# A two-block transformer kernel on one Trainium2 core: the second block's output projection as seven half-size products, its gated mix by token halves

## Chip, core and metric

The kernel runs on one core of one Trainium2 chip. The metric is the device time of one execution in microseconds (us). The engines have names in the profile: PE is TensorE (matmuls), PEld its weight loads, DVE is VectorE, ACT ScalarE, POOL GpSimd, and SP is the engine whose queue issues most of the DMAs. "L80" is line 80 of the kernel file.

## What is computed

Two blocks run one after the other on a sequence of 1024 tokens with 1024 channels, all in float32. The first block has a windowed attention layer and a multiscale pooling layer. The second has, in front of its tokens, 16 meta tokens, then a mixer of two branches, a gated mix, an output projection and an MLP. What concerns the change is this part of the reference:

```python
y_na = neighbourhood_attention(...) @ w_na_out[l]
y_hg = hgrn2_branch(...) @ w_hg_out[l]
mix = jax.nn.sigmoid(gate_na) * y_na + jax.nn.sigmoid(gate_hg) * y_hg
h = h + mix @ w_o[l]
m = rms_norm(h, norm_mlp[l])
h = h + jnp.square(jax.nn.relu(m @ w_up[l])) @ w_down[l]
```

`w_hg_out` is 512 x 1024 and `w_o` is 1024 x 1024.

## The kernel before

**Products.** A float32 product is made of three fp32r matmuls. Each operand is split into a high part (a cast on ACT) and a low part (the original minus the high part), and `mm3` adds high x high, high x low and low x high into one PSUM bank. Low parts of activations are made on DVE (`split_evac`, L118 and L119); low parts of weights on POOL (`split_w`, L79 the cast, L80 the subtraction). A raw weight tile (`wraw`), its high part (`whi`) and its low part (`wlo`) have 128 x 1024 elements and three buffers each.

**The gated mix.** `mixed(e)` makes two of the eight 128-channel blocks of the mix, transposed (channels on partitions), for all tokens. `pair_cols` loads two column blocks of `w_hg` and splits them. For each block and each half of 512 tokens, two pieces of 256 KB are loaded from DRAM into a slot of the tile `fa`: the sigmoid gate (`d_gate`) and the finished first term (`d_y`). Twelve matmuls make the second branch's output in a PSUM bank; DVE multiplies it by the gate (L1359), adds the first term (L1360), and ACT and DVE split the sum into `mh` and `ml`.

**The output projection.** `add_out` multiplies the blocks of the mix by two row blocks of `w_o` at a time and adds each 128 x 512 result to the residual `X` (L539; the first time the residual is also scaled by `rfin`, L541). `X` is two tiles, `Xa` for rows 0 to 3 of 128 tokens and `Xb` for rows 4 to 7. So the two kinds of work alternate: mix of blocks 0 to 3, projection of 0 and 1, mix of 4 and 5, projection of 2 and 3, mix of 6 and 7, and at last the projection of 4 to 7, first for `Xa`, then for `Xb`, for which `w_o`'s rows 4 to 7 are loaded and split a second time. `last_hook` stores finished rows to `d_x` (L1372), and beside the last quarter it makes the norm of rows 0 to 3 and turns them for the MLP.

**After it** the MLP's up projection starts (`first_two`, sums of operands at L1519 and L1533, the seven-product scheme), with the norms of rows 4 to 7 in two pairs (`norms`, L1322 to L1328). The MLP's down projection is written with the helpers `load_d`, `less`, `split_a`, `split_b`, `times` and `into` (L1643 to L1696).

**What sets the order.** Each engine executes its instructions in one fixed order, and each DMA queue in its own. That order comes from the program and from a scheduler that places instructions by their dependences and estimated times; an instruction waits for the semaphores of its inputs and of the buffer that it overwrites, and whatever is queued behind it on its engine waits too.

Of the kernel before, what the change touches and what calls it, by code (L numbers as in the profile page):

```python
# [9 lines left out]
F32 = mybir.dt.float32  # L10
# [9 lines left out]
P = 128  # L20
# [10 lines left out]
def fused_kernel(tc, a, out, stop=None, dbg=None):  # L31
# [4 lines left out]
    def f(x):  # L36
        return x.bitcast(F32)
# [1301 lines left out]
    with ExitStack() as ph:  # L1339
        gp = ph.enter_context(tc.tile_pool(name="gp", bufs=2))  # L1340
        sgs = itertools.count()

        def mixed(e):

            mx, wh = [], pair_cols(w_hg, e)
            for i in range(2):
                m_h = gp.tile([P, T], F32R, name="mh", bufs=4)
                m_l = gp.tile([P, T], F32R, name="ml", bufs=4)
                mx.append((m_h, m_l))
                for hf in range(2):  # L1350
                    sl = slice(hf * 512, hf * 512 + 512)
                    sg = []
                    for src in (d_gate[8 + e + i], d_y[e + i]):
                        g_ = fa[:, next(sgs) % 8, :]
                        nc.sync.dma_start(out=g_, in_=src[:, sl])
# [3 lines left out]
                    nc.vector.tensor_tensor(out=sg[0], in0=ps, in1=sg[0], op=ALU.mult)  # L1359
                    nc.vector.scalar_tensor_tensor(out=sg[0], in0=sg[1], scalar=0.5, in1=sg[0], op0=ALU.mult,  # L1360
                                                   op1=ALU.add)
# [45 lines left out]

    def copy_out(ps):  # L1410
# [19 lines left out]
    def load_d(dst, j, n, c):  # L1430
        for i in range(2):
            q = 4 * c + 2 * i
            loads[:] = [nc.sync.dma_start(out=dst[i], in_=wd[:, q:q + 2, j, n * 512:n * 512 + 512])]
        return dst

    def load_w11(c):
        return load_d([wpool.tile([P, 1024], F32, name="wraw", bufs=3).rearrange("p (k c) -> p k c", k=2)
                       for _ in range(2)], 0, 0, c)

    def load_w2(c):  # L1440
        wx = xt.tile([P, KT, 512], F32, name="xh1")
        w12, w22 = [[wx[:, 4 * n + 2 * i:4 * n + 2 * i + 2, :] for i in range(2)] for n in range(2)]
        load_d(w22, 1, 1, c)
        load_d(w12, 0, 1, c)
        return w12, w22

    blocks = [fa[:, 0:4, :], fa[:, 4:8, :]]
    loads, stores = [None], []

    with ExitStack() as ph:  # L1450
# [17 lines left out]
        def first_two(p, w_):  # L1468
# [3 lines left out]
            u11 = copy_out(b_)  # L1472
# [89 lines left out]
        def pair(p, r1, r2, tt=None):  # L1562
# [45 lines left out]
        w11 = load_w11(0)  # L1608
# [3 lines left out]
    with ExitStack() as ph:  # L1612
# [36 lines left out]
        def load_w21(c):  # L1649
            return load_d([bb.tile([P, 2, 512], F32, name="wb") for _ in range(2)], 1, 0, c)  # L1650
# [5 lines left out]
        def less(out_, x_, y_):  # L1656
            for i in range(2):
                nc.vector.tensor_tensor(out=out_[i], in0=x_[i], in1=y_[i], op=ALU.subtract)  # L1658

        def split_a(n):  # L1660
            t_ = xt.tile([P, KT, 512], F32R, name=("xh0", "xl0", "xl1")[n % 3])
            for i in range(2):
                h, l = t_[:, 2 * i:2 * i + 2, :], t_[:, 4 + 2 * i:6 + 2 * i, :]
                split_evac(h, l, blocks[n % 3][:, 2 * i:2 * i + 2, :])
# [3 lines left out]
        def split_b(b_):
            res = []
            for i in range(2):  # L1670
                hi = wpool.tile([P, 1024], F32R, name="whi").rearrange("p (k c) -> p k c", k=2)
                lo = wpool.tile([P, 1024], F32R, name="wlo").rearrange("p (k c) -> p k c", k=2)
                split_evac(hi, lo, b_[i], nc.gpsimd)
                res.append((hi, lo))
            return res

        def times(banks, s_, w_, first, by_t=False):
            for i, t in [(i, t) for t in range(4) for i in range(2)] if by_t else [(i, t) for i in range(2) for t in range(4)]:
                tsl = slice(t * P, (t + 1) * P)
                mm3(banks[t], [((s_[:, 2 * i + k, tsl], s_[:, 4 + 2 * i + k, tsl]), (w_[i][0][:, k, :], w_[i][1][:, k, :]))  # L1680
                               for k in range(2)], first and i == 0, i == 1, chain=True)
# [92 lines left out]
```

## Time and profile before

| what | value |
| --- | --- |
| three runs | 2376.79, 2378.60, 2380.87 us (median 2378.6) |
| profiled execution | 2379.78 us |
| its span, first to last instruction | 2378.0 us |
| mean granted TensorE clock | 0.994 |
| matmuls | 12102 |
| DMA traffic | 168.68 MB read from HBM, 59.24 MB written |

The page has the span in 40 slices, with each engine's busy share in tenths:

```profile
PE   7999999999999999999999999999989999999997
DVE  5566676654367255553265746767684444786775
ACT  5344452422226454553232232421365555533334
POOL 2112133112126244431212112112354444444455
```

A 9 is 90% or more. One slice is 59.5 us; the changed stage, from the mix to the end of the output projection (1591 to 1735 us), lies in slices 27 to 30.

### The profile page before, as it was taken

To read this page: it belongs to the slowest core of one execution; us is meant where nothing else is said; L and a number is where in the kernel's file an instruction comes from. 1 tells how busy PE (TensorE), PEld (TensorE's weight loads), DVE (VectorE), ACT (ScalarE), POOL (GpSimd) and SP (SyncE) were. 2 spreads that over 40 slices of the span, in tenths; PEclk is the share of its full clock that TensorE was granted. 3 is DMA by queue.
4 is the path that set the end of the run, shared out by engine and by line. 5 is a ranking of instruction groups with operands and counts; after the bars stand their busy time and mean duration, and the time that the engine had idled before them with its cause. 6 is when DMAs were issued, how large, how long until landed. Compare 5 with 4: busy or idle time off the path is not lost. (4 is left out here: it accounts for less than half of the span.)

```text
span 2378.0 us, 32146 instructions
## 1 busy us (share of the span) xinstructions
PE 2317.6 (97%) x12102; PEld 1929.5 (81%) x12102; DVE 1409.7 (59%) x2623; ACT 961.9 (40%) x1788; POOL 762.4 (32%) x516
## 2 busy tenths in 40 slices
PE   7999999999999999999999999999989999999997
PEld 6877777888887888878988888878867888878886
DVE  5566676654367255553265746767684444786775
ACT  5344452422226454553232232421365555533334
POOL 2112133112126244431212112112354444444455
PEclk9999999999999999999999999999999999999999
DMA  5111003111114222211111111465335444754231
GB/s 160 36 28 36 28 27 108 40 45 58 40 59 136 68 67 67 54 58 45 45 53 54 41 54 54 136 217 200 133 102 199 147 150 164 274 213 173 102 124 72
DMA packets 234012, 230.02 MB, mean 97 GB/s; under 512 B 59832, under 2 KB 174862, under 8 KB 230272
## 3 DMA queue, kind: packets, MB, share of 16 engines
q1 hardware_dynamic: 225040, 210.31, 27.7%
q10 hardware_dynamic: 8224, 16.00, 1.8%
q0 software_dynamic: 592, 1.65, 0.3%
q8 instruction: 96, 1.57, 0.3%
q14 instruction: 60, 0.49, 0.1%
HBM read 168.68 MB, written 59.24 MB: 96 GB/s over the span
## 5 line engine op out<-in xcount | busy, mean ns | idle before, releaser
L108 PE MATMUL mm<-xh,whi 128*128 128x512 f32 (+2 forms) x1744 | 671.7, 385 | 8.4 <-DVE st L1418 2.5
L110 PE MATMUL mm<-xl,whi 128*128 128x512 f32 (+2 forms) x1744 | 666.2, 382 | 0.0
L111 PE MATMUL mm<-xh,wlo 128*128 128x512 f32 (+2 forms) x1744 | 662.4, 380 | 1.6 <-POOL wlo L80 1.6
L80 POOL TENSOR_TENSOR wlo<-wraw,whi 128x1024 fp32r<-128x1024 f32 (+1 forms) x135 | 319.8, 2374 | 949.1 <-ACT whi L79 910.4
L108 PEld LDWEIGHTS mm<-xh,whi 128*128 128x128 f32 x1744 | 329.5, 189 | 70.6 <-issue 4.2
L111 PEld LDWEIGHTS mm<-xh,wlo 128*128 128x128 f32 x1744 | 329.6, 189 | 65.6 <-POOL wlo L80 2.7
L110 PEld LDWEIGHTS mm<-xl,whi 128*128 128x128 f32 x1744 | 329.7, 189 | 56.4 <-DVE xl L119 0.3
L79 ACT CAST whi<-wraw 128x1024 fp32r<-128x1024 f32 (+1 forms) x135 | 137.4, 1022 | 386.1 <-PE mm L110 159.9
L111 PE MATMUL mm<-whi,xl 128*128 128x512 f32 (+1 forms) x624 | 221.4, 355 | 0.0
L108 PE MATMUL mm<-whi,xh 128*128 128x512 f32 (+1 forms) x496 | 172.1, 347 | 2.4 <-DVE X L281 1.6
L110 PE MATMUL mm<-wlo,xh 128*128 128x512 f32 (+1 forms) x496 | 171.9, 347 | 1.6 <-POOL wlo L119 1.0
L111 PEld LDWEIGHTS mm<-whi,xl 128*128 128x128 f32 x624 | 117.8, 189 | 16.6
L1553 POOL TENSOR_TENSOR wlo<-raw,whi 128x1024 fp32r<-128x1024 f32 (+1 forms) x42 | 84.3, 2007 | 101.9 <-ACT whi L1552 101.9
L108 PE MATMUL mm<-whi,xl 128*128 128x512 f32 x288 | 112.3, 390 | 1.5 <-ACT whi L118 1.1
L110 PE MATMUL mm<-wlo,xl 128*128 128x512 f32 x288 | 112.1, 389 | 0.0
L108 PEld LDWEIGHTS mm<-whi,xh 128*128 128x128 f32 x496 | 93.7, 189 | 14.5 <-DVE X L281 2.0
L110 PEld LDWEIGHTS mm<-wlo,xh 128*128 128x128 f32 x496 | 93.7, 189 | 13.5 <-POOL wlo L119 1.4
L111 PE MATMUL mm<-whi,ml 128*128 128x512 f32 x256 | 99.7, 392 | 1.6 <-DVE ml L119 1.6
L108 PE MATMUL mm<-whi,mh 128*128 128x512 f32 x256 | 100.4, 392 | 0.1
L110 PE MATMUL mm<-wlo,mh 128*128 128x512 f32 x256 | 99.9, 390 | 0.0
L1479 DVE TENSOR_TENSOR st<-st 128x512 f32<-128x512 f32 x64 | 63.2, 1008 | 58.0 <-ACT st L1465 56.9
L1696 DVE TENSOR_TENSOR X<-X,mm 128x512 f32<-128x512 f32 x112 | 73.1, 681 | 37.4 <-PE mm L111 37.4
(344 smaller groups left out, 4362.6 us busy)
## 6 DMA issues: line engine op xcount, KB each, us to landing
wraw<-in_w_in_dram SPq DMA_DIRECT2D x48, 512.0 KB, 3.9
d_S<-st SPq DMA_DIRECT2D x64, 256.0 KB, 4.6
raw<-in_w_up_dram SPq DMA_DIRECT2D x30, 512.0 KB, 5.4
d_A<-st ACTq DMA_DIRECT2D x48, 256.0 KB, 2.0
fa<-d_S SPq DMA_DIRECT2D x10, 1024.0 KB, 5.4
wraw<-in_pool_w_in_dram SPq DMA_DIRECT2D x18, 512.0 KB, 4.1
fa<-d_A SPq DMA_DIRECT2D x9, 1024.0 KB, 4.9
wraw<-in_attn_w_in_dram SPq DMA_DIRECT2D x32, 256.0 KB, 3.3
```

Of the source, the lines that this page charges most:

```text
L79: nc.scalar.copy(out=hv[:, i:i + n], in_=view[:, i:i + n])
L80: nc.gpsimd.tensor_tensor(out=lv[:, i:i + n], in0=view[:, i:i + n], in1=f(hv[:, i:i + n]), op=ALU.subtract)
L108: nc.tensor.matmul(ps, lhsT=lh[0], rhs=rh[0], start=first and i == 0, stop=False, skip_group_check=chain)
L110: nc.tensor.matmul(ps, lhsT=lh[0], rhs=rh[1], start=False, stop=False, skip_group_check=chain)
L111: nc.tensor.matmul(ps, lhsT=lh[1], rhs=rh[0], start=False, stop=last and i == n - 1, skip_group_check=chain)
L1479: return nc.vector.tensor_tensor(out=out_, in0=x_, in1=y_, op=op)
L1553: nc.gpsimd.tensor_tensor(out=lv, in0=view, in1=f(hv), op=ALU.subtract)
L1696: added[:] = [nc.vector.tensor_tensor(out=dst, in0=dst, in1=banks[t], op=ALU.add)]
```

## The change

The mix keeps its arithmetic, but is made by token halves: `mixed(e, hf)` makes two channel blocks for 512 tokens, for all e of the first half and then of the second, so the pairs of `w_hg` are loaded and split eight times, not four. The gate and the first term go into slots of one staging tile (`stb`, ten slots, also used by the MLP), and the sum goes to a place where it stays: `fa` for the first token half, the new tiles `a21` and `a22` for the second.

The output projection is then one 2 x 2 block product by the seven-product scheme (Strassen's, in Winograd's form with chained sums): tokens, inner channels and output channels are halved, and the four quarters of the mix and of `w_o` (w11, w12, w21, w22, 512 x 512 each) are combined by additions before, and by chained PSUM sums after. Each of the seven products takes 48 matmuls. The helpers of the MLP's down projection are moved up and shared (`load_d`, `less`, `split_b`, `times`, and `split_into` for operand splits on ACT and DVE). The sums of activations are made by `block` on DVE, one of them (a21 + a22) on POOL. `add_x` adds finished quarters to `X`; `summed` stores finished rows; the norm of rows 0 to 3 stands between products 5 and 6 in the text, and their turning (`turn`) between the row tiles of the seventh product. `load_x` loads the residual's rows after some of the mix's steps. The other edits pass arguments for the shared helpers and the staging slot that a pair of the MLP holds.

```diff
-    def stage():
-        return st.tile([P, 512], F32, name="st", bufs=10)
+    stb = st.tile([P, 10, 512], F32, name="st")
+    def stage(hold=None):
+        i = next(i for i in (n % 10 for n in sts) if i not in held.values())
...
+    def split_b(b_):
+        res = []
+        for i in range(2):
+            hi, lo = [wpool.tile([P, 1024], F32R, name=n).rearrange("p (k c) -> p k c", k=2) for n in ("whi", "wlo")]
+            split_evac(hi, lo, b_[i], nc.gpsimd)
+            res.append((hi, lo))
+        return res
...
-        def mixed(e):
-            mx, wh = [], pair_cols(w_hg, e)
+        a21, a22, w12, w22 = [mp.tile([P, 4, 512], F32, name=n) for n in ("a21", "a22", "w12", "w22")]
+        mix = {(0, 0): fa[:, 0:4, :], (0, 1): fa[:, 4:8, :], (1, 0): a21, (1, 1): a22}
+        def mixed(e, hf):
+            wh, sl = pair_cols(w_hg, e), slice(hf * 512, hf * 512 + 512)
             for i in range(2):
...
-                    split_evac(m_h[:, sl], m_l[:, sl], sg[0])
+                g_, y_ = stage(), stage()
+                nc.sync.dma_start(out=g_, in_=d_gate[8 + e + i][:, sl])
+                nc.sync.dma_start(out=y_, in_=d_y[e + i][:, sl])
+                ps, m_ = bank(), mix[hf, i][:, e // 2, :]
+                mm3(ps, [(wh[i][k], oo.at(4 + k, sl)) for k in range(4)])
+                nc.vector.tensor_tensor(out=m_, in0=ps, in1=g_, op=ALU.mult)
+                nc.vector.scalar_tensor_tensor(out=m_, in0=y_, scalar=0.5, in1=m_, op0=ALU.mult, op1=ALU.add)
+        def add_x(banks, h, ch, first=True):
+            for t in range(4 * h, 4 * h + 4):
+                dst, ps = X[ALL, t, slice(ch * 512, ch * 512 + 512)], banks[t - 4 * h]
+                if first:
+                    nc.vector.scalar_tensor_tensor(out=dst, in0=dst, scalar=rfin[:, t:t + 1], in1=ps, op0=ALU.mult,
                                                    op1=ALU.add)
+                else:
+                    nc.vector.tensor_tensor(out=dst, in0=dst, in1=ps, op=ALU.add)
+                if h and not ch:
+                    summed(t)
...
-        m0 = mixed(0)
-        m1 = mixed(2)
...
-        add_out(psm, terms(m0), wo(0), scale=rfin)
-        m0 = mixed(4)
-        add_out(psm, terms(m1), wo(2), by_ch=True)
-        m1 = mixed(6)
-        for hf in range(2):
...
-            add_out(psm, terms(m0), wo(4), tiles=tiles, by_ch=True)
-            w6 = wo(6)
...
-            add_out(psm, terms(m1), w6, last_hook, tiles=tiles)
+        s2, w21 = stb[:, 0:4, :], halves(stb[:, 4:8, :])
+        for e in range(0, KT, 2):
+            mixed(e, 0)
+            if e >= 4:
+                load_d(w22 if e == 4 else w12, wv, int(e == 4), 1)
+        a11, a12 = mix[0, 0], mix[0, 1]
+        o11 = split_a("xh0", halves(a11))
+        mixed(0, 1)
+        load_x(0, 1)
+        o12 = split_a("xl0", halves(a12))
+        mixed(2, 1)
+        load_x(2, 3)
+        mixed(4, 1)
+        w11 = load_w11(wv)
+        mixed(6, 1)
+        load_d(w21, wv, 1, 0)
+        load_x(4, 5, 6, 7)
+        ops = split_b(w11)
+        B, A_ = banks4(), banks4()
+        block(a11, a21, a11, ALU.subtract)
+        times(B, o11, ops, True)
+        ops = split_b(w21)
+        block(a21, a21, a22, ALU.add, nc.gpsimd)
+        less(w12, w12, w22)
+        block(s2, a22, a11, ALU.add)
+        add_x(B, 0, 0)
+        times(A_, o12, ops, True)
+        less(w11, w11, w12)
+        o22 = split_a("xh1", halves(a22))
+        ops = split_a("xl1", halves(s2)), split_b(w11)
+        less(w21, w21, w11)
+        less(w11, w22, w11)
+        add_x(A_, 0, 0, False)
+        times(B, *ops, False)
+        ops = split_a("xh0", halves(a21)), split_b(w11)
+        block(a12, a12, s2, ALU.subtract)
+        add_x(B, 0, 1)
+        C = banks4()
+        times(C, *ops, True)
+        ops = split_a("xl0", halves(a12)), split_b(w22)
+        add_x(C, 1, 1)
+        times(C, *ops, False)
+        ops = split_a("xl1", halves(a11)), split_b(w12)
...
+        add_x(C, 0, 1, False)
+        for t in range(4):
+            summed(t)
+        norms(0, 4)
+        times(B, *ops, False, True)
+        wu0 = load_w(cols(w_up, 0))
+        add_x(B, 1, 1, False)
+        for t, ks in enumerate(((0, 1, 2), (3, 4, 5), (6, 7), ())):
+            times(B, o22, t4, False, True, [t])
+            for k in ks:
+                turn(k)
+        wu0 = split_w(wu0.rearrange("p (k c) -> p k c", k=KT), [KT, P])
+        add_x(B, 1, 0)
```

The lines that the next paragraphs name are, in the changed kernel: L60 a weight load, L1404 and L1405 the loads of gate and first term, L1408 and L1409 the two operations of the mix, L1358 a load of `w_o`, L1367 `less`, L1416 and L1419 `add_x`, L1438 `load_x`, L1448 `block`.

SP's queue at the start of the mix. Before, the loads for the mix (`fa`, L1355) stand between the last stores of the first term (`d_y`, L1240):

```order
L60 DMA wraw<-in_w_hg_out_dram 128x4x128 x2
L1236 DMA gate<-d_gate 128x512
L1240 DMA d_y<-gate 128x512 x2
L1355 DMA fa<-d_gate 128x512
L1240 DMA d_y<-gate 128x512
L1355 DMA fa<-d_y 128x512
L1355 DMA fa<-d_gate 128x512
```

and in the changed kernel (`st` is a slot of the staging tile):

```order
L60 DMA wraw<-in_w_hg_out_dram 128x4x128 x2
L1236 DMA gate<-d_gate 128x512
L1240 DMA d_y<-gate 128x512 x4
L60 DMA wraw<-in_w_hg_out_dram 128x4x128 x2
L1404 DMA st<-d_gate 128x512
L1405 DMA st<-d_y 128x512
L1404 DMA st<-d_gate 128x512
```

All four stores come first now, and another pair of `w_hg` stands ahead of the mix's first load. Further on in the same queue of the changed kernel stand `w12` (here with a number as `w_14792`), the rows of `Xa`, and the `w_hg` pair of e = 4 for the second token half:

```order
L1358 DMA w_14792<-in_w_o_dram 128x2x512 x2
L1404 DMA st<-d_gate 128x512
L1405 DMA st<-d_y 128x512
L1404 DMA st<-d_gate 128x512
L1405 DMA st<-d_y 128x512
L1438 DMA Xa<-d_h 128x1024 x2
L1404 DMA st<-d_gate 128x512
L1405 DMA st<-d_y 128x512
L1404 DMA st<-d_gate 128x512
L1405 DMA st<-d_y 128x512
L1438 DMA Xa<-d_h 128x1024 x2
L60 DMA wraw<-in_w_hg_out_dram 128x4x128 x2
```

That pair now stands behind `w22`, `w12`, four rows of `Xa` and the pieces of twelve of the sixteen products of the mix.

POOL's order from the mix on. Before, it has nothing but low parts of weights up to the MLP's sums (L1532):

```order
L1113 TENSOR_TENSOR kc<-K 128x512 x2
L80 TENSOR_TENSOR wlo<-wraw,whi 128x1024 x6
L1113 TENSOR_TENSOR kc<-K 128x512 x2
L80 TENSOR_TENSOR wlo<-wraw,whi 128x1024 x23
L1532 TENSOR_TENSOR fa<-xh_15758,xl_15759 128x512 x4
```

and in the changed kernel (`a_14790` is `a21`, `a_14791` is `a22`, `w_14793` is `w22`):

```order
L80 TENSOR_TENSOR wlo<-wraw,whi 128x1024 x12
L1448 TENSOR_TENSOR a_14790<-a_14790,a_14791 128x1024
L80 TENSOR_TENSOR wlo<-wraw,whi 128x1024 x2
L119 TENSOR_TENSOR wlo<-wraw,whi 128x1024 x2
L119 TENSOR_TENSOR wlo<-st,whi 128x1024
L1448 TENSOR_TENSOR a_14790<-a_14790,a_14791 128x1024
L119 TENSOR_TENSOR wlo<-st,whi 128x1024
L119 TENSOR_TENSOR wlo<-wraw,whi 128x1024 x4
L119 TENSOR_TENSOR wlo<-w_14793,whi 128x1024 x2
```

The first half of a21 + a22 now stands between the low parts of the first six `w_hg` pairs and those of the last two (e = 4 and e = 6 of the second token half).

DVE's order in the mix. Before, each block's product, sum and low part follow one another:

```order
L1359 TENSOR_TENSOR fa<-mm,fa 128x512
L1360 SCALAR_TENSOR_TENSOR fa<-fa 128x512
L119 TENSOR_TENSOR ml<-fa,mh 128x512
L1359 TENSOR_TENSOR fa<-mm,fa 128x512
L1360 SCALAR_TENSOR_TENSOR fa<-fa 128x512
```

and in the changed kernel, from the seventh sum of the first token half on (`xh_14962` and `xl_15010` are the split halves of the mix for products 1 and 2):

```order
L1409 SCALAR_TENSOR_TENSOR fa<-st,fa 128x512
L1367 TENSOR_TENSOR w_14792<-w_14792,w_14793 128x1024
L1408 TENSOR_TENSOR fa<-mm,st 128x512
L119 TENSOR_TENSOR xh_14962<-fa,xh_14962 128x1024
L1409 SCALAR_TENSOR_TENSOR fa<-st,fa 128x512
L119 TENSOR_TENSOR xh_14962<-fa,xh_14962 128x1024
L1408 TENSOR_TENSOR a_14790<-mm,st 128x512
L119 TENSOR_TENSOR xl_15010<-fa,xl_15010 128x1024
L1409 SCALAR_TENSOR_TENSOR a_14790<-st,a_14790 128x512
L1408 TENSOR_TENSOR a_14791<-mm,st 128x512
L119 TENSOR_TENSOR xl_15010<-fa,xl_15010 128x1024
```

The subtraction w12 - w22 now stands ahead of the eighth product's operations, and low parts of twice the width lie between the products.

More of the change, by code (lines that the diff above doesn't have):

```diff
@@ L1311, in bank @@
         return psm.tile([P, 512], F32, name="mm")
-    def stage():
-        return st.tile([P, 512], F32, name="st", bufs=10)
+    stb = st.tile([P, 10, 512], F32, name="st")
+    sts, held = itertools.count(), {}
+    def stage(hold=None):
+        i = next(i for i in (n % 10 for n in sts) if i not in held.values())
+        if hold is not None:
+            held[hold] = i
+        return stb[:, i, :]
     def norms(t0, n):
@@ new lines, in fused_kernel, with load_d, load_w11, less @@
+    added, loads = [None], [None]
+    def load_d(dst, w, j, n, c=0):
+        for i in range(2):
+            q = 4 * c + 2 * i
+            loads[:] = [nc.sync.dma_start(out=dst[i], in_=w[:, q:q + 2, j, n * 512:n * 512 + 512])]
+        return dst
+    def load_w11(w, c=0):
+        return load_d([wpool.tile([P, 1024], F32, name="wraw", bufs=3).rearrange("p (k c) -> p k c", k=2)
+                       for _ in range(2)], w, 0, 0, c)
+    def less(out_, x_, y_):
+        for i in range(2):
+            nc.vector.tensor_tensor(out=out_[i], in0=x_[i], in1=y_[i], op=ALU.subtract)
@@ new lines, in split_into, with times @@
+    def split_into(t_, parts):
+        for i in range(2):
+            split_evac(t_[:, 2 * i:2 * i + 2, :], t_[:, 4 + 2 * i:6 + 2 * i, :], parts[i])
+        return t_
+    def split_b(b_):
+        res = []
+        for i in range(2):
+            hi, lo = [wpool.tile([P, 1024], F32R, name=n).rearrange("p (k c) -> p k c", k=2) for n in ("whi", "wlo")]
+            split_evac(hi, lo, b_[i], nc.gpsimd)
+            res.append((hi, lo))
+        return res
+    def times(banks, s_, w_, first, by_t=False, rows=range(4)):
+        for i, t in [(i, t) for t in rows for i in range(2)] if by_t else [(i, t) for i in range(2) for t in rows]:
+            tsl = slice(t * P, (t + 1) * P)
+            mm3(banks[t], [((s_[:, 2 * i + k, tsl], s_[:, 4 + 2 * i + k, tsl]), (w_[i][0][:, k, :], w_[i][1][:, k, :]))
+                           for k in range(2)], first and i == 0, i == 1, chain=True)
@@ L1442, in load_w2 @@
         w12, w22 = [[wx[:, 4 * n + 2 * i:4 * n + 2 * i + 2, :] for i in range(2)] for n in range(2)]
-        load_d(w22, 1, 1, c)
-        load_d(w12, 0, 1, c)
+        load_d(w22, wd, 1, 1, c)
+        load_d(w12, wd, 0, 1, c)
         return w12, w22
     blocks = [fa[:, 0:4, :], fa[:, 4:8, :]]
-    loads, stores = [None], []
+    stores = []
     with ExitStack() as ph:
@@ L1599, in pair @@
                 store(order)
+            held.pop(p)
             return n1, n2
@@ L1654, in load_x @@
                 nc.sync.dma_start(out=X[:, t, ch * 512:ch * 512 + 512], in_=d_x[t][:, ch * 512:ch * 512 + 512])
-        def less(out_, x_, y_):
-            for i in range(2):
-                nc.vector.tensor_tensor(out=out_[i], in0=x_[i], in1=y_[i], op=ALU.subtract)
         def split_a(n):
[L1661 to L1664, printed above, removed]
+            t_ = split_into(xt.tile([P, KT, 512], F32R, name=("xh0", "xl0", "xl1")[n % 3]),
+                            [blocks[n % 3][:, 2 * i:2 * i + 2, :] for i in range(2)])
             load_a(n + 3)
             return t_
[L1668 to L1681, printed above, removed]
         w21 = load_w21(0)
@@ L1708, in fused_kernel @@
             n, last = 7 * c, c == NCH - 1
-            B, A_ = [[bank() for _ in range(4)] for _ in range(2)]
+            B, A_ = banks4(), banks4()
             times(B, *ops, True)
@@ L1722, in fused_kernel @@
             into(B, 0, 1)
-            C = [bank() for _ in range(4)]
+            C = banks4()
             times(C, *ops, True)
```

86 lines of the change are left out of this document (33 added, 53 removed).

## The prediction

> **What bounds the kernel now.** I read the page's totals first, then the windows by stage, then the waits of TensorE, and last the timeline of single engines around the gated mix.
>
> ```profile
> span 2378.0 us, 32146 instructions
> PE 2317.6 (97%) x12102; PEld 1929.5 (81%) x12102; DVE 1409.7 (59%) x2623; ACT 961.9 (40%) x1788; POOL 762.4 (32%) x516
> ...
> 1591.00:1667.00 76.00, 75.97 (x333) 62.53 (x334) 51.56 (x67) 13.61 (x19) 16.76 (x7) 1.00 0.62 214
> ...
> 1610.00:1620.00 10.00, 10.00 (x45) 8.26 (x44) 8.49 (x11) 2.82 (x4) 2.39 (x1) 1.00 1.01 379
> ```
>
> TensorE (PE) is the bound: 97% of the span, and without a gap in the changed stage from 1591 to 1667 us. There one matmul takes 75.97/333 = 0.228 us. The last two figures of a window's row are the DMA share and GB/s: at share 1.01 the engines are full, and 379 GB/s is what full means here.
>
> ```profile
> PE mm L1336 <- DVE xl L1519: 2.3, 1, 2.3
> PE mm L1336 <- DVE Xb L1328: 1.5, 1, 1.5
> PE mm L1336 <- DVE st L1418: 0.9, 1, 0.9
> PE mm L108 <- DVE gate L1239: 0.9, 1, 0.9
> PE mm L108 <- ACT st L1522: 0.9, 1, 0.9
> PE mm L111 <- POOL wlo L80: 0.5, 1, 0.5
> ```
>
> Those are all waits of PE from 1590 to 1760. Only the 0.9 at L1239 (before the mix) and the tail behind the output projection (L1328, L1519, L1418, L1522, together 5.6) exist. Whatever the change saves in matmuls is thus real time, unless a new wait appears.
>
> **What the change saves.** The projection has 384 matmuls before (8 row tiles x 2 column halves x 8 row blocks of w_o x 3) and 7 x 48 = 336 after: 48 x 0.228 = **-10.9 us**. The mix keeps its 192 matmuls, but the projection no longer lies between its parts: all 16 mix products, 12 matmuls or 2.74 us each, now run in a row from 1591.0 to 1634.8, so their loads, 11.5 MB and more, must come in 44 us where they were spread over 60.
>
> **What the loads do.**
>
> ```profile
> 1587.77 0.32 SPq L1355 DMA_DIRECT2D fa<-d_gate  x1
> ...
> fa<-d_gate SPq DMA_DIRECT2D x12, 256.0 KB, 4.1
> ...
> 1591.14 2.40 POOL L80 TENSOR_TENSOR wlo<-wraw,whi 128x1024 fp32r<-128x1024 f32 x1 [12.46 <-ACT whi L79]
> ...
> SPq L60 <- POOL wlo L80: 12.6, 3, 8.9
> ...
> wraw<-in_w_hg_out_dram SPq DMA_DIRECT2D x4, 256.0 KB, 7.5
> ...
> wraw<-in_w_o_dram SPq DMA_DIRECT2D x4, 512.0 KB, 3.5
> ```
>
> The row of SP's waits says that its queue stands at a weight load (L60) until GpSimd (POOL) has read the old contents. In the new order such a reload, the w_hg pair of e=2 for the second half, stands ahead of every gate load. It waits for the POOL operation of 1591.14, so until 1593.5, so the gate loads start there and not at 1587.77. With the 4.1 of a gate block the first lands at 1597.7. Product 0 was read at 1594.1 (L1359, next rows), so the vector engine (DVE) starts some 4 us late, which eight PSUM banks (22 us of matmuls) absorb: 0. What they don't absorb is the w_hg pair of e=4, second half. Ahead of it and with it the queue has 11 MiB = 11.5 MB: 24 gate and y blocks (6 MiB), w22 and w12 of w_o (2), four row blocks of Xa (2) and two w_hg pairs (1). At the full 379 GB/s it lands at 1593.6 + 30.4 + 1.5 = 1625.5, where 1.5 is assumed for the way of the last block; at 333, the mean of 287 and 379 in the windows 1600 to 1620, at 1629.7. I take 1628.
>
> ```profile
> 1600.00:1610.00 10.00, 10.00 (x45) 8.15 (x44) 7.83 (x10) 2.87 (x4) 2.41 (x1) 1.00 0.82 287
> ...
> 1594.09 0.69 DVE L1359 TENSOR_TENSOR fa<-mm,fa 128x512 f32<-128x512 f32 x1 [3.21 <-PE mm L111]
> ...
> 1596.86 0.69 DVE L119 TENSOR_TENSOR ml<-fa,mh 128x512 fp32r<-128x512 f32 x1 [1.35 <-ACT mh L118]
> 1597.47 0.69 DVE L1359 TENSOR_TENSOR fa<-mm,fa 128x512 f32<-128x512 f32 x1
> ...
> 1603.33 2.41 POOL L80 TENSOR_TENSOR wlo<-wraw,whi 128x1024 fp32r<-128x1024 f32 x1 [9.79 <-ACT whi L79]
> ...
> 1603.61 2.67 DVE L1360 SCALAR_TENSOR_TENSOR fa<-fa 128x512 f32<-128x512 f32 x1
> ...
> L1658 DVE TENSOR_TENSOR wb<-wb,wraw 128x1024 f32<-128x1024 f32 x8 | 9.7, 1218 | 5.1 <-POOL wlo L119 5.1
> L79 ACT CAST whi<-wraw 128x1024 fp32r<-128x1024 f32 x17 | 17.7, 1051 | 40.3 <-PE mm L111 38.2 <-PE mm L110 2.1
> ```
>
> **First new wait, on the weight of e=4, second half.** PE wants it at 1591.0 + 146 x 0.228 = 1624.3 (its low part is read by the third matmul). After landing it needs a cast (1.05) and POOL's subtraction (2.4): by the loads alone 1628 + 3.45 = 1631.5. A second chain ends later. On DVE the subtraction w12 - w22 (L1367) stands ahead of the last first-half products and of the casts' low parts; w12's first half comes with 6.3 MB: 1611.7 at 379, 1614.0 at 333, I take 1613.6. From there to the sum of product 11 DVE has 7 operations of 128x1024 at 1.22 and 10 of 128x512 at 0.60 (the spacing 1596.86 to 1597.47): 14.5, so 1628.1. POOL's new addition a21 + a22 (L1448) waits for that sum, is queued ahead of the subtraction, and takes 2.4: 1630.5, then the weight's 2.4: **1632.9**. PE waits 1632.9 - 1624.3 = **8.6**, I take 8.5. Its bounds: if DVE is never late, product 11 ends at 1591.0 + 144 x 0.228 = 1623.8, its two DVE operations at 1625.2, POOL's two at 1630.0: 5.7. With w12 at 1614.0 and two of DVE's operations held for 0.7 each by something, 10.
>
> **Second, and the clock.** The pair of e=6 uses the buffer that POOL frees at 1632.9: issue and landing 4.3 (near the 3.5 of the w_o row), cast 1.05, subtraction 2.4: 1640.7. PE is there at 1632.9 + 24 x 0.228 = 1638.4: 2.3. But after a pause the clock falls:
>
> ```profile
> 1740.00:1750.00 10.00, 5.93 (x25) 4.16 (x24) 9.94 (x10) 4.78 (x10) 6.71 (x4) 0.84 0.40 110
> 1750.00:1760.00 10.00, 10.00 (x37) 7.99 (x36) 9.60 (x13) 7.68 (x13) 6.18 (x4) 0.82 0.83 229
> ...
> 1750.41 0.63 PE L110 MATMUL mm<-xl,whi 128*128 128x512 f32 x1
> 1750.84 0.63 PE L111 MATMUL mm<-xh,wlo 128*128 128x512 f32 x1
> ...
> 1754.19 0.39 PE L111 MATMUL mm<-xh,wlo 128*128 128x512 f32 x1
> 1754.42 0.40 PE L108 MATMUL mm<-xh,whi 128*128 128x512 f32 x1
> ```
>
> Granted clock 0.84 and 0.82 over 20 us are (0.16 + 0.18) x 10 x 2 = 6.8 us at half speed, matmuls 0.43 apart for 0.23. After 8.5 us of pause 6.8 us hold 16 matmuls, 0.2 late each: 3.2, which then swallows the 2.3. I take **2.5** for both (2.3 to 3.2). The Trainium skill (TensorE: Matmul & The Clock Gate, Part 1: The HAM clock gate) has the clock back after one busy window of about 3.4 us; by that 8 matmuls lose 1.6 and 0.7 of the wait is left, 2.3 in all. The trace's 6.8 disagrees, so the rows decide.
>
> **Third to fifth, in products 2, 3 and 4.** The work beside PE changes its kind. DVE loses 16 low parts and 36 of 64 additions into X (52 x 0.69 = 36) and gets 30 operations of 128x1024 (30 x 1.22 = 37): the same time. But additions that read PSUM become operations with SBUF inputs alone. In the rows below the addition at 1692.68 reads PSUM and is not held by POOL's operation (0.69); L1360 above took 2.67 because POOL ran from 1603.33 to 1605.74.
>
> ```profile
> 1691.14 2.40 POOL L80 TENSOR_TENSOR wlo<-wraw,whi 128x1024 fp32r<-128x1024 f32 x1 [3.04 <-ACT whi L79]
> ...
> 1692.68 0.69 DVE L539 TENSOR_TENSOR Xa<-Xa,mm 128x512 f32<-128x512 f32 x1 [0.67 <-PE mm L111]
> ...
> L1658 DVE TENSOR_TENSOR xh<-xh 128x1024 f32<-128x1024 f32 x8 | 16.1, 2038 | 0.0
> ...
> L1322 ACT ACTIVATE junk<-Xa 128x1024 bf16<-128x1024 f32 x4 | 4.2, 1058 | 5.5 <-DVE Xa L539 5.5
> ```
>
> POOL has 22 operations for 16 (8 w_hg, 12 of w_o, two additions). From the mix's start to the middle of product 4 there are 16 POOL operations (38.6) and on DVE 16 sums (11.0) and 26 of 128x1024 (31.7) that exclude one another: 81.3 us, where PE's 360 matmuls take 82.1. Product 1 starts at 1634.8 + 8.5 + 2.5 = 1645.8. From the 1640.7 above POOL and DVE go in turns: POOL's two low parts of w11 with DVE's w11 - w12 between and behind, to 1648.0; POOL's w21, first half, 1650.4; DVE's last sums and three wide operations around POOL's second L1448 (2.4), 1658.2; the next a22 + a11, a low part, ScalarE's casts and POOL's w21, second half, 1663.1. PE wants it a product and a half later, at 1645.8 + 72 x 0.228 + 0.5 = 1662.7: 0.4 late. Counted on in the same way, the weight for the middle of product 3 ends at 1675.9 for 1674.1 (1.8), that of product 4 about 0.8 late: **3.0** (0 to 10). The Trainium skill (SBUF — State Buffer, "Who interferes with whom") calls the shared pair of DVE and GpSimd an exclusive lock, the loser blocked for the whole instruction. The 2.67 agrees. With sharing instead these 3.0 would be nought and the sum +0.1.
>
> **The rest.** Products 5 to 7 have no new operand sums on DVE and one POOL operation per half product (2.4 in 5.5 us): 0. The norm of rows 0 to 3 stands beside products 6 and 7 (11 us each) as it stood beside the last quarter before: 0; without this cover it would cost its 4 squares, 1.06 each, and the newton steps. The rows Xa (L1438) are asked for behind products 8 and 10 and wanted at 1651, Xb at product 4, 1683; w21 waits for stage slots that the sums of products 12 and 13 free at about 1640, lands some 4 later and is cast at 1645.8: 0. Two MiB less of w_o (8 loads of 512 KB for 12) and two more of w_hg: the bytes are equal. The tail has a wait less (L1418, L1522: 1.8) and a DVE operation more ahead of L1519, held by POOL (2.3 to about 4.2): 0, between -3 and +3 since it touches all 5.6 and the clock.
>
> **Sum.** -10.9 + 8.5 + 2.5 + 3.0 + 0 = **+3.1**. The profiled execution took 2379.8 us (span 2378.0), 1.2 above the median 2378.6: 2379.8 + 3.1 - 1.2 = 2381.7, say **2382**.
>
> **Rivals.**
> 1. Faster: the loads run full, DVE is never late, and the tail loses the waits at L1418 and L1522 (1.8) with nothing in their place: -10.9 + 5.7 + 1.5 (second wait, landing 3.5) + 0 - 1.8 = -5.5, **2373**. For it: share 1.01 in 1610 to 1620. Against: 287 GB/s in the window before, and DVE's chain of 14.5. Chance 0.19.
> 2. Slower: the turns of DVE and POOL decide. If DVE is behind when product 1 starts, each wait in products 2 to 4 grows and is not made up (81.3 of 82.1 has no slack): the 10 of its bound instead of 3.0, so 2382 + 7 = **2389**. It decides from about 4.7 us in products 2 to 4 (over 2383.4). For it: the mean of 2.04 for L1658 on xh, the same operation held by POOL; against: additions from PSUM fill the turns. Chance 0.23.
> 3. Slower by the clock: waits of 8.5 and then of 2 to 3 in products 2 to 4, as short as those of the tail (2.3, 0.9, 0.9) that halved the clock, drop it a second time: 3 more, **2385**. Chance 0.16.
> 4. The savings are not there, because the matmuls are not on the path: excluded by 75.97 of 76.00.
>
> **Chances and range.** About 0.2% (4.8 us) is what a measurement of this kernel tells from no change: the middle, 2373.8 to 2383.4, holds the forecast (0.42). Rival 1 lies below (0.19), rivals 2 and 3 above (0.39). Range: 2371, rival 1 with 2 us of tail, to 2391, rival 2 with 3.
>
> **What would show it.** PE: one gap of 5 to 10 at 1624 on POOL's wlo, 24 matmuls at a lower clock, then one under 2.5; three small ones on wlo in products 2 to 4; DVE's first L1367 at about 1613.6 and L1448 on POOL from 1628 to 1630.5. The forecast is wrong if the w_hg pair lands before 1621, or if DVE waits for nothing from 1600 on.

## The result, and the profile after

| | median us | runs | ratio to the kernel before, 95% interval |
| --- | --- | --- | --- |
| before | 2380.36 | 7 | |
| changed | 2388.19 (2383.08 to 2391.14) | 7 | 1.0035 [1.0023, 1.0047] |

The changed kernel is slower by 0.35%, some 8 us, inside the stated range but outside the middle case that the forecast of 2382 stood for. The profiled execution took 2383.08 us, the shortest of the seven. Its page:

```profile
span 2380.9 us, 32015 instructions
PE 2307.8 (97%) x12054; PEld 1919.5 (81%) x12054; DVE 1418.9 (60%) x2601; ACT 969.8 (41%) x1792; POOL 783.0 (33%) x522
```

48 matmuls and 9.8 us of PE's busy time are gone, and the span is longer all the same. Where the mix starts in either trace is the first row of PE that waits for `gate` (L1239); of the changed kernel:

```profile
1587.40 0.47 PE L108 MATMUL mm<-xh,whi 128*128 128x512 f32 x1 [0.87 <-DVE gate L1239]
```

Before, the same row stands at 1591.03. The 3.6 us between them arose ahead of the change, and they fit the spread of single executions: in the profiles of the experiments below the row stands anywhere from 1588.03 to 1591.68. So the profiles are compared from there: 2378.0 - 1591.03 = 787.0 us before, 2380.9 - 1587.40 = 793.5 after, **+6.5**. The runs' medians say +7.8; the other 1.3 are not in this profile, which is of the shortest run.

The waits of PE from the mix to the end of the output projection, of the changed kernel (total, times, longest):

```profile
PE mm L108 <- ACT whi L79: 5.6, 1, 5.6
PE mm L110 <- POOL wlo L119: 4.0, 3, 1.8
PE mm L108 <- DVE Xb L1416: 3.8, 2, 2.0
PE mm L111 <- POOL wlo L80: 1.2, 1, 1.2
```

Before, there was no wait in that stage. Rows of all four, in order of time:

```profile
1620.39 0.39 PE L111 MATMUL mm<-xh,wlo 128*128 128x512 f32 x1
1626.43 0.79 PE L108 MATMUL mm<-xh,whi 128*128 128x512 f32 x1 [5.65 <-ACT whi L79]
...
1628.87 0.80 PE L111 MATMUL mm<-xh,wlo 128*128 128x512 f32 x1 [1.22 <-POOL wlo L80]
1629.46 0.63 PE L108 MATMUL mm<-xh,whi 128*128 128x512 f32 x1
1629.89 0.63 PE L110 MATMUL mm<-xl,whi 128*128 128x512 f32 x1
...
1631.95 0.39 PE L108 MATMUL mm<-xh,whi 128*128 128x512 f32 x1
...
1659.06 0.50 PE L110 MATMUL mm<-wlo,xl 128*128 128x512 f32 x1 [1.33 <-POOL wlo L119]
...
1691.66 0.47 PE L108 MATMUL mm<-whi,xl 128*128 128x512 f32 x1 [2.00 <-DVE Xb L1416]
...
1695.04 0.50 PE L108 MATMUL mm<-whi,xl 128*128 128x512 f32 x1 [1.77 <-DVE Xb L1416]
```

The first two waits (5.65 and 1.22) are PE idle for the `w_hg` pair of e = 4, second half, 6.9 us in all. Until 1631.95 the matmuls there start 0.43 us apart, where 0.23 is usual: half speed. The waits on POOL's low parts of L119 lie in the middles of products 2, 3 and 4, those on `Xb` at the start of product 5. What the pair waited for, on ACT, POOL and DVE:

```profile
1610.04 1.23 DVE L1367 TENSOR_TENSOR w<-w,w 128x1024 f32<-128x1024 f32 x1 [1.46 <-DMA w<-in_w_o_dram]
...
1623.40 0.69 DVE L1409 SCALAR_TENSOR_TENSOR a<-st,a 128x512 f32<-128x512 f32 x1
...
1624.16 2.34 POOL L1448 TENSOR_TENSOR a<-a,a 128x1024 f32<-128x1024 f32 x1 [16.12 <-DMA st<-d_gate]
1626.46 2.35 POOL L80 TENSOR_TENSOR wlo<-wraw,whi 128x1024 fp32r<-128x1024 f32 x1
...
1625.33 1.05 ACT L79 CAST whi<-wraw 128x1024 fp32r<-128x1024 f32 x1 [10.64 <-DMA wraw<-in_w_hg_out_dram]
```

ACT had stood idle 10.64 us when the load landed at 1625.2; the cast ended at 1626.4. POOL's addition a21 + a22 came right behind DVE's sum of product 11, which ended at 1624.09 (its row names an older DMA as the releaser), and ended at 1626.5, at the same moment as the cast. Two chains tie, and this trace alone doesn't tell which one must go.

### The profile page after: what moved, and what is told of

It is laid out like the page before. It is cut to its first block, busy times and chain, and to the rows that moved or that the text cites. A ratio compares the mean times of both kernels' runs of the same rounds, so it can differ in the third digit from the quotient of the medians.

```text
span 2380.9 us, 32015 instructions
## 1 busy us (share of the span) xinstructions
PE 2307.8 (97%) x12054; PEld 1919.5 (81%) x12054; DVE 1418.9 (60%) x2601; ACT 969.8 (41%) x1792; POOL 783.0 (33%) x522
## 5 line engine op out<-in xcount | busy, mean ns | idle before, releaser
L80 POOL TENSOR_TENSOR wlo<-wraw,whi 128x1024 fp32r<-128x1024 f32 (+1 forms) x127 | 301.6, 2380 | 881.4 <-ACT whi L79 827.8
L111 PE MATMUL mm<-whi,xl 128*128 128x512 f32 (+1 forms) x688 | 246.1, 358 | 0.0
L110 PE MATMUL mm<-wlo,xh 128*128 128x512 f32 (+1 forms) x528 | 184.2, 349 | 2.5 <-POOL wlo L119 1.9
L108 PE MATMUL mm<-whi,xh 128*128 128x512 f32 (+1 forms) x528 | 184.5, 349 | 1.1 <-ACT ona L907 0.6
L111 PEld LDWEIGHTS mm<-whi,xl 128*128 128x128 f32 x688 | 129.8, 189 | 19.1
L108 PE MATMUL mm<-whi,xl 128*128 128x512 f32 x352 | 137.5, 391 | 5.4 <-DVE Xb L1416 3.8
L110 PE MATMUL mm<-wlo,xl 128*128 128x512 f32 x352 | 137.2, 390 | 3.1 <-POOL wlo L119 3.1
L119 POOL TENSOR_TENSOR wlo<-wraw,whi 128x1024 fp32r<-128x1024 f32 x30 | 79.8, 2665 | 80.0 <-ACT whi L118 80.0
L878 DVE CUSTOM_DVE_ANT_0 s<-S,bi 128x400 f32<-128x400 f32 x64 | 34.5, 571 | 94.5 <-PE S L870 94.5
L119 DVE TENSOR_TENSOR pl<-PT,ph 100x512 fp32r<-100x512 f32 (+2 forms) x128 | 83.6, 668 | 10.2 <-ACT ph L118 9.1
```

The lines of the kernel that those rows point to most:

```text
L80: nc.gpsimd.tensor_tensor(out=lv[:, i:i + n], in0=view[:, i:i + n], in1=f(hv[:, i:i + n]), op=ALU.subtract)
L108: nc.tensor.matmul(ps, lhsT=lh[0], rhs=rh[0], start=first and i == 0, stop=False, skip_group_check=chain)
L110: nc.tensor.matmul(ps, lhsT=lh[0], rhs=rh[1], start=False, stop=False, skip_group_check=chain)
L111: nc.tensor.matmul(ps, lhsT=lh[1], rhs=rh[0], start=False, stop=last and i == n - 1, skip_group_check=chain)
L119: (lo_eng or nc.vector).tensor_tensor(out=lo, in0=src, in1=f(hi), op=ALU.subtract)
L878: nc.vector.tensor_tensor_reduce(out=s, in0=sps[j], in1=bs[j], scale=-0.125, scalar=-NEG, op0=ALU.add, op1=ALU.min, accum_out=mx)
```

## Experiments

Each kernel was timed 5 to 11 times beside the kernel before. "From the mix" is the time from the mix's first matmul to the end in its profile (before 787.0, changed 793.5). 

**Xa's rows later.**

```diff
         mixed(0, 1)
-        load_x(0, 1)
         o12 = split_a("xl0", halves(a12))
         mixed(2, 1)
-        load_x(2, 3)
...
-        load_x(4, 5, 6, 7)
+        load_x(*range(8))
```

> Edit: the four rows of Xa are asked for behind the last mix step, not behind its products 8 and 10; the first half of a21 + a22 thereby falls behind the low part of the w_hg pair of e = 4, second half, on POOL. In the changed kernel that pair lands 37.8 us after the mix's start and PE waits 6.9 us for it (5.65 for the high part, 1.22 for the low). Theory 'late loads': 2 MiB less ahead at about 390 GB/s land it 5.4 us sooner, at 32.4; cast to 33.5, low part to 35.9, PE is there at 33.4: a wait of about 2 us, no clock drop behind it, and 5 to 6 us less than the changed kernel, about 2383 (ratio to the kernel before about 1.001). Rival 'DVE's chain and the addition on POOL set it': the wait stays near 7 and so does the time, 2388 (ratio 1.0035).

Median 2383.96, ratio 1.0016 [1.0007, 1.0025]; from the mix 789.4. ACT and POOL of this kernel, whose mix starts at 1590.50:

```profile
1622.98 1.05 ACT L79 CAST whi<-wraw 128x1024 fp32r<-128x1024 f32 x1 [4.30 <-DMA wraw<-in_w_hg_out_dram]
...
1624.11 3.82 POOL L80 TENSOR_TENSOR wlo<-wraw,whi 128x1024 fp32r<-128x1024 f32 x1 [13.31 <-ACT whi L79]
```

The pair lands 32.4 us after the mix's start, as expected, and the waits of 5.65 and 1.22 become 0.20 and 2.70. The low part took 3.82 and not 2.4: from 1623.9 to 1625.7 DVE ran two operations whose inputs all lie in SBUF, and the 1.4 more are about the time that POOL's spent beside them. That the clock would not drop was expected wrongly: behind the wait of 2.70, 14 matmuls ran at half speed, from the first of these rows to the second, with no wait between:

```profile
1627.98 0.80 PE L111 MATMUL mm<-xh,wlo 128*128 128x512 f32 x1 [2.70 <-POOL wlo L80]
...
1634.12 0.42 PE L108 MATMUL mm<-xh,whi 128*128 128x512 f32 x1
```

**The sum a21 + a22 on DVE.**

```diff
-        block(a21, a21, a22, ALU.add, nc.gpsimd)
+        block(a21, a21, a22, ALU.add)
```

> Edit: a21 + a22 is made by DVE, not by POOL, so nothing stands ahead of the low part of the w_hg pair of e = 4, second half, on POOL; the loads stay as in the changed kernel. Theory 'late loads': landing still 37.8 us after the mix's start, cast to 38.9, low part to 41.3 us, the same wait of 6.9 us; time within 2 us of the changed kernel's 2388 (two more wide operations on DVE, two fewer on POOL in products 1 and 2). Rival 'the addition on POOL sets it': the low part comes 2.3 us sooner and the wait falls to about 4.6.

Median 2388.50, ratio 1.0030 [1.0018, 1.0041]; from the mix 796.3. PE's waits in the mix:

```profile
PE mm L108 <- ACT whi L79: 6.2, 1, 6.2
PE mm L111 <- POOL wlo L80: 1.2, 1, 1.2
```

The wait stays. POOL now has nothing ahead of the low part and starts it as soon as the cast is done:

```profile
1630.91 2.35 POOL L80 TENSOR_TENSOR wlo<-wraw,whi 128x1024 fp32r<-128x1024 f32 x1 [19.34 <-ACT whi L79]
```

So the landing of the load sets the wait, and POOL's addition only happened to end with it.

**Splits for products 6 and 7 later.**

```diff
-        ops = split_a("xl1", halves(a11)), split_b(w12)
+        ops = split_a("xh0", halves(a11)), split_b(w12)
-        t4 = list(zip(*[halves(mp.tile([P, 4, 512], F32R, name=n)) for n in ("a22", "w22")]))
+        t4 = list(zip(*[halves(mp.tile([P, 4, 512], F32R, name=n)) for n in ("a22", "w12")]))
```

> Edit: the splits of the operands of product 6 and of product 7's weight write into other buffers (xh0 for xl1, w12 for w22), which come free later; on DVE they thereby stand behind the four additions into Xb (L1416) that read product 4's banks, not ahead of and between them. Theory 'queue on DVE': the waits of PE on Xb at product 5 (2.00, 1.77, 0.14 = 3.9 us) vanish, nothing else moves: about 2384 (ratio 1.0019). Rival: the additions are late because DVE is full from before, then most of the 3.9 stays: 2387 or more.

Median 2381.79, ratio 1.0008 [0.9999, 1.0017]; from the mix 789.9, 3.6 less than the changed kernel. The waits up to the end of the projection:

```profile
PE mm L108 <- ACT whi L79: 5.6, 1, 5.6
PE mm L110 <- POOL wlo L119: 2.6, 2, 1.7
PE mm L111 <- POOL wlo L80: 1.3, 1, 1.3
```

The line with L1416 is gone, and nothing took its place at product 6. What stood there in the changed kernel, on DVE and POOL:

```profile
1684.37 6.48 DVE L119 TENSOR_TENSOR xl<-fa,xl 128x1024 fp32r<-128x1024 f32 x2
1690.78 0.73 DVE L1416 SCALAR_TENSOR_TENSOR Xb<-Xb,rfin,mm 128x512 f32<-128x512 f32 x1
1691.44 2.89 DVE L119 TENSOR_TENSOR w<-st,a 128x1024 fp32r<-128x1024 f32 x1
1694.25 0.73 DVE L1416 SCALAR_TENSOR_TENSOR Xb<-Xb,rfin,mm 128x512 f32<-128x512 f32 x1
...
1684.04 5.73 POOL L119 TENSOR_TENSOR wlo<-w,whi 128x1024 fp32r<-128x1024 f32 x2
```

Two low parts for product 6 (3.2 us each beside POOL's) stood ahead of the first addition into Xb, one for product 7 (2.9, beside POOL's of 1690.87) between the first and the second. Product 5 adds into the very banks that these additions read, so PE waits for each.

**The mix by pairs of blocks** (token halves undone; the splits of a11 and a12, which are complete only at the mix's end now, move behind it).

```diff
+        whs = {}
         def mixed(e, hf):
-            wh, sl = pair_cols(w_hg, e), slice(hf * 512, hf * 512 + 512)
+            if e not in whs:
+                whs[e] = pair_cols(w_hg, e)
+            wh, sl = whs[e], slice(hf * 512, hf * 512 + 512)
...
         for e in range(0, KT, 2):
             mixed(e, 0)
...
+            if e < 6:
+                mixed(e, 1)
```

> Edit: token halves are undone alone: for each pair of blocks both token halves are made with one load and one split of w_hg (four pairs, not eight), the seven products stay. Theory 'late loads': no wait of PE in the mix (8.5 us of wait and half clock less); POOL has four operations fewer up to product 4, so by 'turns of DVE and POOL' the waits in the middle of products 2, 3 and 4 (1.33, 1.76, 0.92 = 4.0) fall to 2 or less; the 3.9 at product 5 stay: 2378 to 2380 (ratio 0.999 to 1.000). Rival 'those waits come from DVE alone': they stay at 4.0, 2381. Rival 'a wait moves to product 1, whose operand a11 is complete only at the mix's end': 2 to 4 us there, 2382 to 2384.

Median 2378.86, ratio 0.9996 [0.9987, 1.0004]; from the mix 785.7.

```profile
PE mm L108 <- DVE Xb L1420: 3.8, 2, 2.2
PE mm L111 <- DVE xl L119: 1.8, 1, 1.8
PE mm L111 <- DVE xh L119: 1.1, 1, 1.1
PE mm L110 <- POOL wlo L119: 0.5, 1, 0.5
```

No wait in the mix is left (L1420 is L1416 here). The small waits of products 1 to 4 fell only from 4.0 to 3.4 and moved, to products 1 and 2 and mostly to DVE's low parts: the "2 or less" missed, as did the rival with 2 to 4 at product 1 (1.1). The moved splits change DVE's order too, so this run does not separate the two.

**Pairs and later splits together.**

> Edit: e4_mix_by_pairs and e3_splits_late together. If the two costs are independent, the 3.9 us of waits on Xb at product 5 go from e4's 785.7 us (mix's start to the end): 782, a median of about 2375 (ratio 0.998). Rival: DVE is so full from product 1 on that the wait comes back at product 6, whose operands are now split later: 2378 or more.

Median 2372.69, ratio 0.9973 [0.9962, 0.9984]; from the mix 782.2, 3.5 less than by pairs alone. The two costs add up, and the kernel is faster than before.

**Low parts of w_o on DVE, with these two.**

```diff
-    def split_b(b_):
+    def split_b(b_, eng=nc.gpsimd):
...
-            split_evac(hi, lo, b_[i], nc.gpsimd)
+            split_evac(hi, lo, b_[i], eng)
...
-        ops = split_b(w21)
+        ops = split_b(w21, nc.vector)
```

(and in the same way at the other five places of the projection.)

> Edit: e5, and the low parts of w_o's quarters and their differences (12 operations of 2.4 us on POOL) are made by DVE (12 of 1.22 = 14.6 us). Theory 'turns of DVE and POOL': DVE is held by POOL no more in products 1 to 6 (operations of 3.4 become 1.2), and the waits there, 3.4 us in e4, fall to 1 or less: about 2372. Rival 'DVE's own work fills the stage': in products 1 to 4 (44 us) DVE has about 24 us of wide operations and 11 of additions by their free durations, with 10 more of low parts 45 us; then the waits grow by several us, 2378 or more.

Median 2370.44, ratio 0.9957 [0.9943, 0.9971]; from the mix 779.1. The waits in products 1 to 5 fell from 4.9 in the run before it to 2.6, not to 1, but the forecast of 2372 held: the fastest kernel of the study. Of the 2.6 that are left 2.2 are on low parts that DVE makes now (`wlo` at L119), so here DVE's own work begins to set the time.

**Only every second of these low parts.**

> Edit: as e6, but only every second low part (6 of the 12) goes to DVE. Both engines have slack then: DVE about 40 of 44 us, POOL 14 us less. Theory 'turns': the holds of DVE halve and the waits of e5 in products 1 to 4 fall by half, 1 to 2 us. Rival 'DVE's own work': 1 to 2 us longer than e5.

Median 2372.63, ratio 0.9970 [0.9960, 0.9980]; from the mix 780.8, and 2.3 us of waits in products 1 to 5. By the trace it lies between the two; by the runs it can't be told from either.

**The norm behind product 7** (on the changed kernel).

```diff
-        norms(0, 4)
         times(B, *ops, False, True)
...
-            for k in ks:
-                turn(k)
...
         add_x(B, 1, 0)
+        norms(0, 4)
+        for k in range(KT):
+            turn(k)
```

> Edit of the changed kernel: the first rows' norm and turning stand behind the seventh product in the text, not beside it; 32 turns of Xa in a row on PE after the last matmul of product 7. Forecast's step 'cover': beside the product they cost nothing. Without the cover PE waits for the last split of the turns (about 2 us) and, where the norm itself is late, for 4 squares of 1.06, the newton steps and 2 scalings (8 us): 3 to 10 us more than the changed kernel, 2391 to 2398. Rival 'the norm is ready early anyway, since it needs only Xa': under 2 us, 2388 to 2390.

Median 2391.40, ratio 1.0049 [1.0036, 1.0062], against 1.0035 [1.0023, 1.0047]: the intervals overlap. From the mix it is 799.1, 5.6 more, of which 1.0 is a longer first wait (6.29 + 1.54). The wait for Xb's norm (L1335) went from 2.4 to 3.6. So the cover is worth some 3 to 5 us, but the runs don't separate that from less.

**Low parts on DVE alone** (on the changed kernel, the same edit as two above).

> Edit of the changed kernel alone: the 12 low parts of w_o's quarters and their differences go from POOL to DVE, token halves and the order of the splits stay. Theory 'turns of DVE and POOL': the waits in the middle of products 2 to 4 (1.33, 1.76, 0.92 = 4.0) fall to 2 or less, and those at product 5 (3.9), where DVE's splits took 3.15, 3.40 and 2.89 beside POOL, to 1 to 2 by the holds that go; the 6.9 in the mix stay: 2383 to 2385 (ratio 1.0015 to 1.002). Rival 'DVE's own work': DVE is 2 to 3 us behind from the late start after the mix's wait, the waits stay or grow: 2388 or more.

Median 2378.77, ratio 0.9998 [0.9989, 1.0007]; from the mix 786.9. The window that holds products 1 to 4 of the changed kernel (columns as in the prediction: PE, PEld, DVE, ACT and POOL busy), then all waits of PE from the mix to the end of the projection in this one, and its window:

```profile
1640.00:1690.00 50.00, 45.65 (x198) 36.45 (x196) 48.24 (x37) 19.95 (x21) 27.34 (x10) 1.00 0.23 72
```

```profile
PE mm L108 <- ACT whi L79: 5.2, 1, 5.2
PE mm L111 <- POOL wlo L80: 1.9, 1, 1.9
```

```profile
1640.00:1690.00 50.00, 50.00 (x223) 41.39 (x222) 50.00 (x54) 21.41 (x21) 6.73 (x1) 1.00 0.27 92
```

Every wait behind the mix is gone, those at product 5 too, though splits still stand ahead of and between the additions into Xb. The forecast had kept some of them and was too high (2383 to 2385). DVE does 54 operations in the time in which it did 37: the 48.24 us of before were to a good part time in which it was held, that is, its operations on SBUF inputs took longer while POOL ran one. A group of L1367, from 1637 to 1697 us, shows it, the changed kernel first:

```profile
L1367 DVE TENSOR_TENSOR wraw<-wraw,w 128x1024 f32<-128x1024 f32 x2 | 6.7, 3408 | 2.3 <-POOL wlo L119 2.3
```

```profile
L1367 DVE TENSOR_TENSOR wraw<-wraw,w 128x1024 f32<-128x1024 f32 x2 | 2.4, 1217 | 0.0
```

The rival, DVE's own work, falls: DVE has twelve operations more, and its first addition into Xb starts 95.3 us after the mix's start (1683.82 - 1588.57) instead of 103.4 (1690.78 - 1587.40). The hold has turned round: the one operation that POOL has left in this window, half of a21 + a22, took 6.73 us for 2.4.

Moving the low parts also spares POOL its 2.4 us each, so one may ask whether POOL was merely slow. In the changed kernel it was not full: it stood idle ahead of each of the three low parts that PE waited for, until ACT had cast the high part.

```profile
1656.60 2.41 POOL L119 TENSOR_TENSOR wlo<-st,whi 128x1024 fp32r<-128x1024 f32 x1 [3.20 <-ACT whi L118]
...
1668.54 5.79 POOL L119 TENSOR_TENSOR wlo<-wraw,whi 128x1024 fp32r<-128x1024 f32 x2 [6.19 <-ACT whi L118]
...
1681.59 2.49 POOL L119 TENSOR_TENSOR wlo<-wraw,whi 128x1024 fp32r<-128x1024 f32 x1 [7.26 <-ACT whi L118]
```

Ahead of these casts in ACT's queue stand casts that wait for sums of DVE, and DVE was late with those by its holds: before the first, for instance, two additions of L1448 took 4.55 us, beside POOL's a21 + a22, where two take 2.36 in this run; before the second, two splits of 1.22 took 2.75 and 2.11; before the third, a difference took 3.39.

**Token halves with the three mends** (Xa later, splits later, low parts on DVE).

> Edit: token halves stay, with the three mends together: Xa's rows later (e1), splits later (e3), low parts on DVE (e9). If the costs are independent: from e6, the same with the mix by pairs, it differs by the wait of about 2.9 us in the mix (e1: 0.20 + 2.70) and the clock behind it (3 us): 2375 to 2377 (ratio 0.998 to 0.999). If token halves cost more than that wait: 2379 or more.

Median 2373.89, ratio 0.9975 [0.9963, 0.9986]; from the mix 784.8 in its profile, which is the slowest of its seven runs.

```profile
PE mm L111 <- POOL wlo L80: 4.0, 2, 2.8
```

What is left up to the end of the projection are the waits for the `w_hg` pairs of e = 4 (1.6) and now e = 6 (3.0), with 0.6 on ACT's high parts among them. Its median, 1 us under the forecast, is 3.5 above that of the mix by pairs with later splits and low parts on DVE, no more than these 4.6 and the half speed behind them (14 matmuls): token halves cost their reload, and nothing else that the runs show.

## Why the prediction was right, and where it failed

The change made the kernel slower, as forecast, and the time lies in the range. Of the mechanisms that the text names, the late load, the half speed and the turns of DVE and POOL all came; one place that it put at nought did not stay there. The terms of its sum, against the traces from the mix's start to the end:

| step | forecast | measured |
| --- | --- | --- |
| 48 matmuls fewer | -10.9 | -10.9 (48 x 0.228; 12102 and 12054 counted) |
| first wait, pair of e = 4 | 8.5 | 6.9 |
| pair of e = 6, and the clock | 2.5 | no wait; about 3.1 left over |
| middles of products 2, 3, 4 | 3.0 | 1.33 + 1.76 + 0.92 = 4.0 |
| products 5 to 7 | 0 | 2.00 + 1.77 + 0.14 = 3.9, all at product 5 |
| tail | 0 | about -0.5 |
| sum | +3.1 | +6.5 |

The tail begins where PE waits for the norm of Xb, before and after:

```profile
1734.81 1.60 PE L1336 MATMUL mm<-ident,Xb 128*128 128x128 f32 x12 [1.48 <-DVE Xb L1328]
```

```profile
1739.10 1.10 PE L1343 MATMUL mm<-ident,Xb 128*128 128x128 f32 x6 [2.42 <-DVE Xb L1335]
```

From there to the end, wait included, are 2378.0 - 1734.81 + 1.48 = 644.7 and 2380.9 - 1739.10 + 2.42 = 644.2 us, so -0.5; from the mix to there 142.3 and 149.3, so +7.0. The 3.1 are what -10.9, 6.9, 4.0 and 3.9 leave of that; nine matmuls 0.2 late are 1.8 of it; the rest, 1.3, was not taken apart.

**The first wait** came as described. From the mix's start the pair landed at 37.8 us (forecast 37.0), w12 at 22.6 (22.6), POOL's addition ended at 39.1 (39.5), and the weight's low part at 41.4 (41.9). It was put too high by 1.6: the chain ended 0.5 sooner, PE came 0.5 later, and the two matmuls ahead of the low part ran at half speed, which takes 0.8 more and counts as work. And 5.65 of it stood on ACT's high part, where the text looked for all of it on POOL's low part. What the text had wrong was the reason: it let POOL's addition a21 + a22 set the end. With that addition off POOL the wait stayed (6.2 + 1.2), with 2 MiB less ahead of the load it fell to 2.9. The addition ended in the same 0.1 us as the cast and hid nothing; that the chain which didn't matter gave nearly the right time is luck. The landing itself, 37.0 for 37.8, was foreseen.

**The clock.** The half speed held to 1631.95 and began, by the windows' granted clock, near 1625:

```profile
1625.00:1630.00 5.00, 2.35 (x5) 1.45 (x6) 0.00 (x0) 1.05 (x1) 3.81 (x2) 0.50 0.70 256
1630.00:1635.00 5.00, 5.00 (x20) 4.05 (x19) 1.38 (x2) 2.00 (x2) 1.41 (x1) 0.81 0.96 284
```

0.50 x 5 + 0.19 x 5, times two, are 6.9 us, as the 6.8 taken from the kernel before. But the text put all of them behind PE's restart, 16 matmuls (24 in its list of signs), and only 5.5 lie there, with the wait of 1.22 in them: nine matmuls. The Trainium skill (TensorE: Matmul & The Clock Gate, Part 1: The HAM clock gate) lets the clock return after about 3.4 us of sustained work. The stretch here is broken by that wait and can't decide it; the unbroken one with Xa's rows later is longer, 6.1 us (1627.98 to 1634.12). The wait on e = 6 was swallowed, as forecast: its low part was done at 1636.5, and PE read it at 1636.6.

**The turns of DVE and POOL** were placed right (all three middles, each on POOL's low part) and sized 3.0 for 4.0. With the low parts on DVE all of it goes; that run alone doesn't separate the hold from POOL's own 2.4 us per operation, but POOL's idle times ahead of the three low parts do: it wasn't full, it came late behind DVE's held sums. The Trainium skill (SBUF — State Buffer, "Who interferes with whom") calls the shared pair an exclusive lock; 1.22 became 3.41 in the group above, near 1.22 and POOL's 2.4 together, and the trace agrees.

**The step that failed** is "products 5 to 7: 0". Its reason, no new sums on DVE there and slack on POOL, looked at how much work stands in that place and not at its order. DVE's order has the two low parts of product 6's operand and one of product 7's weight ahead of and between the four additions into Xb, which product 5 waits for since it goes on in their banks; held by POOL, these splits took 3.2 and 2.9 us each. This is the turns' mechanism once more, in a place where the text had left it out: 3.9 us. Both remedies, other order or no hold, bring it to nought.

**Rivals.** By its own words the second (the turns decide, slower) did not come: products 2 to 4 waited 4.0, under the 4.7 from which it was to decide. With the 3.9 at product 5 its mechanism cost 7.9, and the time came out near its 2389; it had named the turns, not that place. A second drop of the clock (the third) is not in the profile: the window from 1640 to 1690 above has a granted clock of 1.00. The faster case needed the loads at full speed, 379 GB/s. From the mix's start to the wait they moved 336 GB/s at a share of 0.94,

```profile
1587.40:1620.78 33.38, 33.38 (x144) 26.93 (x144) 21.67 (x27) 7.18 (x8) 10.15 (x4) 1.00 0.94 336
```

and the pair landed 3.3 us behind the 34.5 that full speed would have given. That the matmuls are off the path stays excluded: with most of the waits mended the saving shows, 2370.4 against 2379.7.

## What to carry to other kernels

Fewer matmuls pay only if the operand work that replaces them fits beside what is left: count, for the stage alone, the operations that read SBUF on both inputs on VectorE and those on GpSimd as one queue, and look in the order for what stands ahead of an addition that frees or feeds a bank. Where that sum comes near the matmuls' time, a low part on VectorE (1.22 us) is cheaper than the same on GpSimd (2.4 us), since there it costs both engines; how far that goes shows in the 2.2 us of waits on DVE's own low parts in the fastest kernel. Reloading a weight for a second pass puts it behind every load that was asked for meanwhile; price it by the bytes ahead of it, not by its own size.

## What the runs showed of the hardware

The hold is mutual: POOL's low part took 3.82 us beside DVE for 2.4, its addition even 6.73 beside a row of DVE's operations, and DVE's operation 3.41 beside POOL for 1.22. A wait of 2.70 us was enough to bring half speed for 14 matmuls, while those of 5.65 and 1.22 brought it for nine. So the length of the wait does not tell how long the half speed lasts behind it.
